# Output projection of a hybrid decoder trunk: its FoX half with seven block products in place of eight

## The chip, the core and the metric

The kernel runs on one core of a Trainium2 chip. The metric is the device time of one execution in microseconds (us), as the median of several runs. A profile of one execution says what each engine did: TensorE (PE, with its weight loads as PEld), VectorE (DVE), ScalarE (ACT), GpSimd (POOL) and the queue SP, which issues most of the DMA transfers.

## The reference

One layer of a decoder trunk, 1024 tokens by 1024 channels, in float32. Cut to what matters here:

```python
def reference(x, p, norm_w, w_in, fox_fb, hgrn_gn, hgrn_lb_logits, w_out, w_ple, w_ple_gate, final_norm_w):
    lb_all = hgrn_lower_bounds(hgrn_lb_logits)
    h = x
    for i in range(DEPTH):                                   # DEPTH = 1
        u = rmsnorm(h, norm_w[i])
        proj = jnp.einsum('bsd,de->bse', u, w_in[i])
        hq, hf, hi, hg, fq, fk, fv, fg, fz = jnp.split(proj, SPLIT_POINTS, axis=-1)
        y_h = hgrn2_branch(hq, hf, hi, lb_all[i], hgrn_gn[i]) * jax.nn.silu(hg)
        y_f = fox_branch(fq, fk, fv, fz, fox_fb[i]) * jax.nn.silu(fg)
        y = jnp.concatenate([y_h, y_f], axis=-1)             # 1024 + 1024 channels
        h = h + jnp.einsum('bse,ed->bsd', y, w_out[i])       # the output projection
        ple = jnp.einsum('bsk,kd->bsd', p[i], w_ple[i])
        h = h + jax.nn.sigmoid(jnp.einsum('bsd,de->bse', h, w_ple_gate[i])) * ple
    return rmsnorm(h, final_norm_w)
```

## The kernel before

Everything is held channels first: a tile has 128 channels as partitions and tokens as columns. The 1024 tokens are worked in two chunks of 512 (`NCH` chunks of `CH`), the channels in eight tiles (`KT`).

To keep float32 precision on TensorE, each operand is split in two parts: a high part (`hi`, a cast by ScalarE, line L82) and a low part (`lo`, source minus high, line L83, by VectorE or GpSimd). Each product of two tiles is three matmuls, high by high (L98), low by high (L99) and high by low (L100); one matmul has 128x128 weights and up to 512 moving columns.

The program's end, where the change lies, has three stages.

1. The HGRN half of the output projection: for each of the eight column tiles `n`, `dense` multiplies the weights of `w_out[n]` by the eight tiles of `y_h` for one chunk after the other (24 matmuls each); `ev_h1` adds x to the result and writes `h[n]` (L1019, VectorE). In the same loop the eight tiles of the FoX output `y_f`, which the earlier stage wrote to memory (`yd`), are read back (L1048) and split into `yhi` and `ylo`.
2. The FoX half: for each column tile `n`, `dense` multiplies `w_out[8+n]` by the tiles of `y_f`, and `ev_h` adds the result to `h[n]` (L1026, VectorE) and splits that chunk at once into `hh` and `hl`, the gates' operands (`hm`). The weights of a tile are loaded and split one tile ahead (`load_w`, two buffers `wf`, two pairs `whi`/`wlo`).
3. The gates: for the token ranges 0 to 512, 512 to 768 and 768 to 1024, and for each column tile, `gate` multiplies `w_gate[n]` by the eight tiles of `hm`, applies a tanh form of the sigmoid, adds the embedding term and sums squares; `norm` ends a range. The gate weights' low parts are made by GpSimd (`wlo`, `glo`, L83); those of the first two tiles, during stages 1 and 2, go into the buffers that the loads of `y_f` had used (tag `g` of the pool `g01`).

What sets the order: each engine works through its own queue in a fixed order, and waits there for semaphores of the others. A scheduler of the framework writes these queues from the program; what is marked to be kept in program order (`pe`, `pin`) stays as written. A buffer of a pool is given out again in turn, and its new writer waits for the old readers. The tiles `hm` use the 32 buffers (tag `u`) that held `y_h`.

Of the kernel before, what the change touches and what calls it, by code (L numbers as in the profile page):

```python
# [64 lines left out]
def trunk(ctx: ExitStack, tc: tile.TileContext, a, out):  # L65
    nc = tc.nc
    mm = nc.tensor.matmul
# [13 lines left out]
    def split(hi, lo, src, lo_engine, pin=lambda ins: ins):  # L81
        pin(nc.scalar.copy(hi, src))  # L82
        pin(lo_engine.tensor_tensor(out=lo, in0=src, in1=hi, op=ALU.subtract))  # L83

    def load_w(src, k, lo_engine=None, pin=lambda ins: ins):

        wf = wpool.tile([P, KT, P], F32, name="wf", tag="wf", bufs=2)
        nc.sync.dma_start(out=wf[:, :k], in_=src)
        hi = wpool.tile([P, KT, P], F32R, name="whi", tag="whi")
        lo = wpool.tile([P, KT, P], F32R, name="wlo", tag="wlo")  # L90
        split(hi[:, :k], lo[:, :k], wf[:, :k], lo_engine or nc.gpsimd, pin)
        return hi, lo

    def product(ps, terms, pin=lambda ins: ins):

        n = len(terms)
        for i, (whi, wlo, uhi, ulo) in enumerate(terms):
            pin(mm(ps, whi, uhi, start=i == 0, stop=False))  # L98
            pin(mm(ps, whi, ulo, start=False, stop=False))  # L99
            pin(mm(ps, wlo, uhi, start=False, stop=i == n - 1))  # L100
# [57 lines left out]
    with ExitStack() as st:  # L158
# [61 lines left out]
        acc = sp.tile([P, S], F32, name="acc")  # L220
# [47 lines left out]
        u = operands("uhi", "ulo")  # L268
# [27 lines left out]
        for c in range(NCH):  # L296
            for k in range(KT):
# [6 lines left out]
                if c == 0 and k in (2, 4, 6, 7):  # L304
                    i = 8 + (2, 4, 6, 7).index(k)
# [59 lines left out]
    pe = tc.keep_in_program_order  # L365
# [142 lines left out]
    with ExitStack() as st:  # L508
# [269 lines left out]
    with fox as st:  # L778
# [219 lines left out]
        for c in range(NCH):  # L998
            sl = slice(c * CH, (c + 1) * CH)
# [4 lines left out]
    with ExitStack() as st:  # L1004
        hpool = st.enter_context(tc.tile_pool(name="h", bufs=1, side="right", reuse_waits="tile"))
        g01 = st.enter_context(tc.tile_pool(name="g01", bufs=4, reuse_waits="tile"))
        eps_ = st.enter_context(tc.tile_pool(name="eps", bufs=2, space=PSUM, reuse_waits="tile"))
# [4 lines left out]
        h = [h_pair[n // 2][:, n % 2] for n in range(KT)]  # L1012

        def ev_h1(n):
            def ev(c, ps):
                sl = slice(c * CH, (c + 1) * CH)
                x = g01.tile([P, CH], F32, name="xr", bufs=2)
                nc.sync.dma_start(out=x, in_=a["xT"][n][:, sl])
                nc.vector.tensor_tensor(out=h[n][:, sl], in0=ps, in1=x, op=ALU.add)  # L1019

            return ev

        def ev_h(n):
            def ev(c, ps):
                sl = slice(c * CH, (c + 1) * CH)
                nc.vector.tensor_tensor(out=h[n][:, sl], in0=ps, in1=h[n][:, sl], op=ALU.add)  # L1026
                split(*hm[c][n], h[n][:, sl], nc.vector)

            return ev

        def load_gate(n, pool, names, **tag):
            wf = wpool.tile([P, KT, P], F32, name="wf", tag="wf", bufs=2)
            nc.sync.dma_start(out=wf, in_=a["w_gate"][n])
            hi, lo = (pool.tile([P, KT, P], F32R, name=name, **tag) for name in names)
            split(hi, lo, wf, nc.gpsimd)
            return hi, lo

        gw = [None] * KT
        with tc.tile_pool(name="yp", bufs=2 * KT, reuse_waits="tile") as yp:

            y_f = [[] for _ in range(NCH)]
            w = [first_w, load_w(a["w_out"][1], KT, nc.vector, tc.keep_in_program_order)]
            for n in range(KT):
                dense(None, y_h, ev_h1(n), w=w[n])
                w.append(load_w(a["w_out"][n + 2], KT, nc.vector, tc.keep_in_program_order))
                hi, lo = (yp.tile([P, S], F32R, name=name, tag="y") for name in ("yhi", "ylo"))
                y = g01.tile([P, S], F32, name="yf", tag="g")
                nc.sync.dma_start(out=y, in_=yd[KT + n])  # L1048
                split(hi, lo, y, nc.vector, tc.keep_in_program_order)
                for c in range(NCH):  # L1050
                    y_f[c].append(tuple(t[:, c * CH : (c + 1) * CH] for t in (hi, lo)))
            for n in range(2):
                gw[n] = load_gate(n, g01, ("ghi", "glo"), tag="g")

            hm = operands("hh", "hl")
            for n in range(KT):
                dense(a["w_out"][KT + n], y_f, ev_h(n), lo_engine=nc.vector, w=w[KT + n] if n < 2 else None)


        gp = st.enter_context(tc.tile_pool(name="gp", bufs=1, reuse_waits="tile"))  # L1060
# [51 lines left out]
        for t0, t1 in ((0, 512), (512, 768), (768, 1024)):  # L1112
            acc = gp.tile([P, t1 - t0], F32, name="acc", bufs=2)
# [53 lines left out]
```

## Time and profile before

| what | value |
|---|---|
| median of 3 runs | 1309.99 us (1309.87 to 1310.46) |
| the profiled execution's own time | 1311.11 us |
| its span, first to last instruction | 1309.4 us |
| mean granted TensorE clock | 0.996 |
| TensorE busy | 1268.6 us, 97% of the span |
| VectorE, ScalarE, GpSimd busy | 787.7, 475.9, 348.8 us |
| FoX half of the output projection | from 1116.1 to 1203.2 us of the span |

A row of a group of instructions names the line, the engine, the operation, output and inputs with buffer numbers left out, the shape, and how often; then busy time and mean, and how long the engine was idle just before and who ended that. A row of the timeline begins with the start and the duration in us. Stretches of the span ("windows") give busy time per engine, the granted TensorE clock (1.00 is full speed), the share of the DMA engines and what they moved.

### The profile page before, as it was taken

Reading aid. Unit: us, or ns where it says so; the run is one execution under the profiler, and the core shown is the slowest. Engines: PE = TensorE matmul, PEld = TensorE weight load, DVE = VectorE, ACT = ScalarE, POOL = GpSimd, SP = SyncE. Lnnn points to the kernel's source line nnn. Section 1 sums busy time; section 2 is a strip of 40 time slices with the busy share of each in tenths; the row PEclk is TensorE's granted clock in tenths of the full one; section 3 lists DMA queues with packets and bytes.
Section 4 is the critical chain, followed back from the end, with each engine's and each line's share of the span. In section 5 each row is a group of like instructions: output and inputs, shape, how many; then the busy total and the mean of one; then the engine's idle time right before and its main releaser. Section 6 shows DMA issues by size and latency. Waiting matters only on the chain.

```text
span 1309.4 us, 26795 instructions
## 1 busy us (share of the span) xinstructions
PE 1268.6 (97%) x10996; PEld 1014.2 (77%) x10996; DVE 787.7 (60%) x1986; ACT 475.9 (36%) x1146; POOL 348.8 (27%) x288
## 2 busy tenths in 40 slices
PE   7999999999999999999999999999999999999995
PEld 5978888888888878776777777776666788888895
DVE  6556575656647475377666665667777733333465
ACT  6423122222313124344444444444545412222454
POOL 3523113112211112433343424232422200102232
PEclk9999999999999999999999999999999999999998
DMA  7411111201111011222222222211232652212321
GB/s 298 141 38 60 50 49 50 66 18 57 42 50 50 20 66 32 83 60 65 66 74 61 71 69 65 71 58 58 81 114 73 221 183 95 81 49 79 116 80 65
DMA packets 38970, 102.22 MB, mean 78 GB/s; under 512 B 6720, under 2 KB 8896, under 8 KB 38848
## 3 DMA queue, kind: packets, MB, share of 16 engines
q1 hardware_dynamic: 38704, 99.99, 22.9%
q8 instruction: 86, 1.41, 0.4%
q0 software_dynamic: 144, 0.52, 0.1%
q14 instruction: 36, 0.29, 0.1%
HBM read 83.07 MB, written 17.43 MB: 77 GB/s over the span
## 4 chain that ended last, share of the span: by engine, by line
PE 82%; DVE 7%; ACT 6%; DMA 2%; issue 2%; POOL 1%; SPq 0%; DVEq 0%; ACTq 0%; POOLq 0%
PE ps L371 47%; PE ps L100 5%; PE lg L823 5%; PE ps L98 5%; PE ps L99 5%; PE po L871 4%; ACT x L859 2%; PE ps L578 1%; PE gps L99 1%; PE gps L98 1%; PE gps L100 1%; PE po L721 1%; PE po L719 1%; DVE x L837 1%; DMA wf<-in_w_in_dram 1%
## 5 line engine op out<-in xcount | busy, mean ns | idle before, releaser
L371 PE MATMUL ps<-uhi,whi 128*128 128x512 f32 x896 | 360.0, 402 | 0.0
L371 PE MATMUL ps<-ulo,whi 128*128 128x512 f32 x896 | 354.3, 395 | 0.0
L371 PE MATMUL ps<-uhi,wlo 128*128 128x512 f32 x896 | 352.6, 393 | 0.0
L83 POOL TENSOR_TENSOR wlo<-wf,whi 128x1024 fp32r<-128x1024 f32 x59 | 145.3, 2462 | 452.8 <-ACT whi L82 423.4
L371 PEld LDWEIGHTS ps<-uhi,whi 128*128 128x128 f32 x896 | 168.2, 188 | 58.5 <-issue 21.6
L371 PEld LDWEIGHTS ps<-uhi,wlo 128*128 128x128 f32 x896 | 168.4, 188 | 35.6 <-issue 1.1
L371 PEld LDWEIGHTS ps<-ulo,whi 128*128 128x128 f32 x896 | 168.4, 188 | 33.5 <-issue 0.7
L82 ACT CAST whi<-wf 128x1024 fp32r<-128x1024 f32 (+1 forms) x77 | 79.7, 1036 | 206.3 <-PE ps L99 90.0
L859 ACT ACTIVATE x<-x,mxo 128x512 f32<-128x512 f32 (+15 forms) x256 | 130.4, 512 | 66.2 <-DVE mxo L847 66.2
L837 DVE CUSTOM_DVE_ANT_0 x<-lg,fb 128x512 f32<-128x512 f32 (+15 forms) x256 | 101.7, 434 | 78.3 <-PE lg L823 71.4
L860 DVE STREAM_TRANSPOSE pt<-x 128x512 f32<-128x512 f32 (+15 forms) x256 | 115.1, 457 | 38.0 <-ACT x L859 33.9
L98 PE MATMUL ps<-yhi,whi 128*128 128x512 f32 x256 | 99.8, 390 | 1.7 <-DVE h L1019 1.7
L99 PE MATMUL ps<-ylo,whi 128*128 128x512 f32 x256 | 99.7, 389 | 0.4 <-DVE ylo L83 0.4
L100 PE MATMUL ps<-yhi,wlo 128*128 128x512 f32 x256 | 99.6, 389 | 0.0
L823 PE MATMUL lg<-k,q 64*32 64x480 f32 (+15 forms) x1024 | 74.4, 396 | 2.6 <-DVE mx L837 2.6
L823 PE MATMUL lg<-k,qx 64*32 64x512 f32 (+15 forms) x1024 | 74.4, 396 | 0.0
L871 PEld LDWEIGHTS po<-pt,v 64*64 64x64 f32 x1536 | 53.8, 133 | 23.0 <-issue 9.2
L871 PE MATMUL po<-pt,v 64*64 64x256 f32 (+7 forms) x1536 | 69.9, 321 | 0.0
L98 PEld LDWEIGHTS ps<-yhi,whi 128*128 128x128 f32 x256 | 48.0, 188 | 12.2 <-ACT whi L82 2.1
L99 PEld LDWEIGHTS ps<-ylo,whi 128*128 128x128 f32 x256 | 48.0, 188 | 10.6 <-DVE ylo L83 0.8
L100 PEld LDWEIGHTS ps<-yhi,wlo 128*128 128x128 f32 x256 | 48.0, 188 | 10.0
L371 PE MATMUL ps<-wthi,uhi 128*128 128x256 f32 x192 | 54.0, 281 | 0.0
(209 smaller groups left out, 2141.2 us busy)
## 6 DMA issues: line engine op xcount, KB each, us to landing
wf<-in_w_in_dram SPq DMA_DIRECT2D x64, 512.0 KB, 3.5
fb<-fd SPq DMA_DIRECT2D x64, 128.0 KB, 3.2
yf<-yd SPq DMA_DIRECT2D x16, 512.0 KB, 5.9
wf<-in_w_out_dram SPq DMA_DIRECT2D x16, 512.0 KB, 3.6
x<-in_xT_dram SPq DMA_DIRECT2D x8, 512.0 KB, 9.4
pled<-pleo SPq DMA_DIRECT2D x16, 256.0 KB, 2.9
yd<-sg SPq DMA_DIRECT2D x8, 512.0 KB, 2.6
rz<-zd SPq DMA_DIRECT2D x16, 256.0 KB, 3.4
```

The source lines that it names most:

```text
L82: pin(nc.scalar.copy(hi, src))
L83: pin(lo_engine.tensor_tensor(out=lo, in0=src, in1=hi, op=ALU.subtract))
L98: pin(mm(ps, whi, uhi, start=i == 0, stop=False))
L99: pin(mm(ps, whi, ulo, start=False, stop=False))
L100: pin(mm(ps, wlo, uhi, start=False, stop=i == n - 1))
L371: pe(mm(ps, x, y, start=i == j == 0, stop=i == n - 1 and j == 2))
L578: pe(mm(ps[32 * j : 32 * j + 32, c * 48 : c * 48 + 48], k[:, 32 * n : 32 * n + 32], mov(n), start=True, stop=True))
L823: mm(ps[32 * j : 32 * j + 32, m % 2, : 32 * n], q[:, 32 * (j // 2) :][:, :32], k[not own][rows].rearrange("p (t a k) -> p t a k", a=2, k=3 ...
L837: nc.vector.tensor_tensor_reduce(out=x, in0=ps[:, m % 2, : 32 * n], in1=copies[m % 2][:, : 32 * n], scale=1.0, scalar=BIG, op0=ALU.add, op ...
L859: nc.scalar.activation(x, x, AF.Exp, bias=self.other[:, g : g + 1], scale=-1.0, accum_out=zs[:, m : m + 1])
L860: nc.vector.transpose(self.probs[:, : m + 1, g], x.rearrange("p (t k) -> p t k", k=32))
L871: mm(po[half[t % 2], r, 32 * first : 256], v_t[self.p][half[r], t ^ r, half[self.i]], self.probs[half[r], t, first:].rearrange("p g q -> p ...
```

## The change

The first two of the eight column tiles of the FoX half are computed as before. The other six are taken in three pairs. For a pair with the weights a (tile n) and b (tile n+1), each cut by input channel into a first half (tiles 0 to 3) and a second half (4 to 7), and y cut in the same halves and into the two chunks of tokens, the four results (2 tiles x 2 chunks) are a 2x2 block product. Written plainly it has eight block products of 4 x 3 = 12 matmuls. The changed kernel uses seven (the Strassen-Winograd form): it forms four sums of blocks of y once, four sums of blocks of weights for each pair, and adds the products together in `h`.

- `sums_y`: for each of four steps k, reads tiles k and k+4 of `y_f` from memory once more (two loads of 512 KB), forms four differences of 128x512 (`tf`; two by VectorE, two by GpSimd) and splits each (cast by ScalarE, low part by VectorE) into `thi` and `tlo`. These take the 32 buffers `u`. The `tf` share three buffers (tag `t`) with `xr` of stage 1, which had two of its own.
- `Seven(n)`: loads the raw weights of a pair into the two buffers `wf`, and forms `s12` and `s34` (four VectorE operations of 128x512, tag `g`). `parts` splits a raw or summed tile into `whi` and `wlo` (still two pairs of buffers; four such tiles w1 to w4 in a pair).
- `run`: the seven products p1, p6, p2, p5, p7, p3, p4, each in one of four PSUM banks, and after each the additions to `h` (VectorE, three a pair by GpSimd from the SBUF tile `acc`). The next pair's loads and sums are written between p7 and p3.
- The gates' operands `hm` are no longer split behind each result. Their 32 buffers are those of `thi`/`tlo`, which are read until the last pair's products are done; `gate_operands` splits them in four groups within the last pair. The loads of the first two gate weights stand behind the last pair, since `s12` and `s34` use their buffers.

The diff, cut:

```diff
         def ev_h1(n):
...
-                x = g01.tile([P, CH], F32, name="xr", bufs=2)
+                x = g01.tile([P, CH], F32, name="xr", tag="t", bufs=3)
...
                 nc.vector.tensor_tensor(out=h[n][:, sl], in0=ps, in1=h[n][:, sl], op=ALU.add)
-                split(*hm[c][n], h[n][:, sl], nc.vector)
...
+        def sums_y(t):
+            for k in range(KT // 2):
+                b1, b2 = (g01.tile([P, S], F32, name="yf", tag="g") for _ in range(2))
+                nc.sync.dma_start(out=b1, in_=yd[KT + k])
+                nc.sync.dma_start(out=b2, in_=yd[KT + KT // 2 + k])
+                b11, b12, b21, b22 = b1[:, :CH], b1[:, CH:], b2[:, :CH], b2[:, CH:]
+                f1, f2, f3, f4 = (g01.tile([P, CH], F32, name="tf", tag="t", bufs=3) for _ in range(4))
+                minus(f1, b12, b11)
+                minus(f2, b22, f1)
+                split(*t[0][k], f2, nc.vector)
+                split(*t[1][k], f1, nc.vector)
+                minus(f3, b22, b12, nc.gpsimd)
+                split(*t[2][k], f3, nc.vector)
+                minus(f4, b21, f2, nc.gpsimd)
+                split(*t[3][k], f4, nc.vector)
...
+            def run(self, w1, w2, t, following, done):
+                nat = [[y_f[c][KT // 2 * r : KT // 2 * r + KT // 2] for c in range(NCH)] for r in range(2)]
+                p1 = self.times(w1, 0, nat[0][0])
+                acc = g01.tile([P, CH], F32, name="acc", tag="t", bufs=3)
+                nc.scalar.copy(acc, p1)
+                self.add(0, 0, p1)
+                p6 = self.times(w2, 0, t[0])
+                nc.vector.tensor_tensor(out=acc, in0=p6, in1=acc, op=ALU.add)
+                self.add(0, 1, acc, nc.gpsimd)
+                done(0)
+                p2 = self.times(w1, 1, nat[1][0])
+                self.add(0, 0, p2)
+                w3 = self.parts(self.s34)
+                p5 = self.times(w2, 1, t[1])
+                self.add(1, 1, p5)
+                self.add(0, 1, p5)
+                done(1)
+                w4 = self.parts(self.raw[1], (1,))
+                p7 = self.times(w3, 0, t[2])
+                nc.vector.tensor_tensor(out=acc, in0=p7, in1=acc, op=ALU.add)
+                self.add(1, 0, acc, nc.gpsimd)
+                self.add(1, 1, acc, nc.gpsimd)
+                done(2)
+                nxt = following and Seven(following)
+                p3 = self.times(w3, 1, nat[1][1])
+                self.add(0, 1, p3)
+                w1 = nxt and nxt.parts(nxt.raw[0])
+                p4 = self.times(w4, 1, t[3])
+                self.add(1, 0, p4)
+                w2 = nxt and nxt.parts(nxt.s12)
+                done(3)
...
-            hm = operands("hh", "hl")
-            for n in range(KT):
-                dense(a["w_out"][KT + n], y_f, ev_h(n), lo_engine=nc.vector, w=w[KT + n] if n < 2 else None)
+            for n in range(2):
+                dense(None, y_f, ev_h(n), w=w[KT + n])
+            t = [[tuple(upool.tile([P, CH], F32R, name=name, tag="u") for name in ("thi", "tlo")) for _ in range(KT // 2)] for _ in range(4)]
+            sums_y(t)
...
+            ready = (
+                [(0, 0), (0, 1), (0, 2), (0, 3)],
+                [(0, 4), (0, 5), (1, 0), (1, 1)],
+                [(1, 2), (1, 3), (1, 4), (1, 5)],
+                [(0, 6), (0, 7), (1, 6), (1, 7)],
+            )
+            seven = Seven(2)
+            w1, w2 = seven.parts(seven.raw[0]), seven.parts(seven.s12)
+            for n in range(2, KT, 2):
+                last = n == KT - 2
+                seven, w1, w2 = seven.run(w1, w2, t, None if last else n + 2, lambda i: gate_operands(*ready[i]) if last else None)
             for n in range(2):
                 gw[n] = load_gate(n, g01, ("ghi", "glo"), tag="g")
```

How the queues move, at the places that the prediction speaks of. First VectorE at the FoX half's start, before: after the last part of y (`ylo`), each result (L1026) is followed by the splits of the gates' operand and of the next weights.

```order
L83 TENSOR_TENSOR ylo_11452<-yf_11453,yhi_11451 128x1024
L1026 TENSOR_TENSOR h0_10902<-ps_11501,h0_10902 128x512
L83 TENSOR_TENSOR hl_11470<-h0_10902,hh_11469 128x512
L1026 TENSOR_TENSOR h0_10902<-ps_11529,h0_10902 128x512
L83 TENSOR_TENSOR wlo_11616<-wf_11613,whi_11615 128x1024
L83 TENSOR_TENSOR hl_11486<-h0_10902,hh_11485 128x512
```

VectorE in the changed kernel, the end of the same stretch: the last step of the sums, with the third of the four results of the two plain tiles among it, up to the split of the first pair's `s12` (`wlo_11690`).

```order
L1031 TENSOR_TENSOR tf_11658<-yf_11654,tf_11657 128x512
L1031 TENSOR_TENSOR ws_11678<-wf_11673,wf_11674 128x512
L1031 TENSOR_TENSOR ws_11678<-wf_11673,ws_11677 128x512
L1026 TENSOR_TENSOR h0_10902<-ps_11509,h0_10902 128x512
L83 TENSOR_TENSOR tlo_11568<-tf_11658,thi_11567 128x512
L83 TENSOR_TENSOR wlo_11684<-wf_11673,whi_11683 128x512
L83 TENSOR_TENSOR tlo_11576<-tf_11657,thi_11575 128x512
L83 TENSOR_TENSOR wlo_11684<-wf_11673,whi_11683 128x512
L83 TENSOR_TENSOR tlo_11584<-tf_11659,thi_11583 128x512
L83 TENSOR_TENSOR tlo_11592<-tf_11660,thi_11591 128x512
L1026 TENSOR_TENSOR h0_10902<-ps_11535,h0_10902 128x512
L83 TENSOR_TENSOR wlo_11690<-ws_11677,whi_11689 128x512 x2
```

From the last result of stage 1 (L1019) to the first of the two operations of that last row, the queue has 31 operations of 128x512 and two of 128x1024; before, the queue from there held one result and one or two splits per chunk.

Then GpSimd, from its last DMA of the FoX stage on, before: the splits of the gate weights alone.

```order
L933 DMA yd_69<-o7_4288 128x1024
L83 TENSOR_TENSOR glo_11460<-wf_11457,ghi_11459 128x1024
L83 TENSOR_TENSOR glo_11466<-wf_11463,ghi_11465 128x1024
L83 TENSOR_TENSOR wlo_11992<-wf_11989,whi_11991 128x1024
L83 TENSOR_TENSOR wlo_11998<-wf_11995,whi_11997 128x1024
```

GpSimd in the changed kernel, from the last subtraction of the sums on:

```order
L1031 TENSOR_TENSOR tf_11660<-yf_11654,tf_11658 128x512
L1083 TENSOR_TENSOR h1_10903<-acc_11708,h1_10903 128x512 x3
L1083 TENSOR_TENSOR h2_10900<-acc_11844,h2_10900 128x512 x3
L83 TENSOR_TENSOR glo_12148<-wf_12145,ghi_12147 128x1024
L1083 TENSOR_TENSOR h3_10901<-acc_11980,h3_10901 128x512
L83 TENSOR_TENSOR glo_12154<-wf_12151,ghi_12153 128x1024
L1083 TENSOR_TENSOR h3_10901<-acc_11980,h3_10901 128x512 x2
L83 TENSOR_TENSOR wlo_12164<-wf_12161,whi_12163 128x1024
L83 TENSOR_TENSOR wlo_12170<-wf_12167,whi_12169 128x1024
```

Eight subtractions of the sums and nine additions of the rounds have come in, and all gate weights' splits stand in the last pair or behind it.

Last VectorE into the gates, before: one split per result, and then the first gate's result (L1078).

```order
L1026 TENSOR_TENSOR h3_10901<-ps_11929,h3_10901 128x512
L83 TENSOR_TENSOR hl_11484<-h3_10901,hh_11483 128x512
L1026 TENSOR_TENSOR h3_10901<-ps_11957,h3_10901 128x512
L83 TENSOR_TENSOR hl_11500<-h3_10901,hh_11499 128x512
L1078 SCALAR_TENSOR_TENSOR g_12053<-g_12053,pl_12026 128x512
```

VectorE in the changed kernel from the result of p7 (L1104) on; `hl_12130` is the low part of the seventh tile of h, first chunk, and the next L1083 is the result of p4, the last product.

```order
L1104 TENSOR_TENSOR acc_11980<-gps_12069,acc_11980 128x512
L83 TENSOR_TENSOR hl_12062<-h0_10902,hh_12061 128x512
L83 TENSOR_TENSOR hl_12086<-h1_10903,hh_12085 128x512
L83 TENSOR_TENSOR hl_12090<-h1_10903,hh_12089 128x512
L1083 TENSOR_TENSOR h3_10901<-gps_12101,h3_10901 128x512
L83 TENSOR_TENSOR hl_12094<-h2_10900,hh_12093 128x512
L83 TENSOR_TENSOR hl_12098<-h2_10900,hh_12097 128x512
L83 TENSOR_TENSOR hl_12130<-h3_10901,hh_12129 128x512
L1083 TENSOR_TENSOR h3_10901<-gps_12115,h3_10901 128x512
L83 TENSOR_TENSOR hl_12134<-h3_10901,hh_12133 128x512
```

The splits that stood behind each result over the whole stage now stand together around the last products; from the result of p2 to `hl_12130` there are 17 operations.

More of the change, by code (lines that the diff above doesn't have):

```diff
@@ L1026, in ev, with minus @@
                 nc.vector.tensor_tensor(out=h[n][:, sl], in0=ps, in1=h[n][:, sl], op=ALU.add)
-                split(*hm[c][n], h[n][:, sl], nc.vector)
             return ev
+        def minus(out, x, y, engine=nc.vector):
+            engine.tensor_tensor(out=out, in0=x, in1=y, op=ALU.subtract)
+        def sums_y(t):
[13 more added lines that the diff above has]
+                split(*t[3][k], f4, nc.vector)
@@ new lines, in trunk, with __init__, parts, times @@
+        class Seven:
+            def __init__(self, n):
+                self.n = n
+                lo, hi = slice(0, KT // 2), slice(KT // 2, KT)
+                self.raw = a_, b_ = [wpool.tile([P, KT, P], F32, name="wf", tag="wf", bufs=2) for _ in range(2)]
+                for i, t in enumerate(self.raw):
+                    nc.sync.dma_start(out=t, in_=a["w_out"][KT + n + i])
+                self.s12, self.s34 = s12, s34 = [g01.tile([P, KT, P], F32, name="ws", tag="g") for _ in range(2)]
+                nc.vector.tensor_tensor(out=s12[:, hi], in0=b_[:, lo], in1=b_[:, hi], op=ALU.add)
+                minus(s12[:, lo], s12[:, hi], a_[:, lo])
+                minus(s34[:, lo], a_[:, lo], b_[:, lo])
+                minus(s34[:, hi], a_[:, hi], s12[:, lo])
+            def parts(self, src, halves=(0, 1)):
+                hi, lo = (wpool.tile([P, KT, P], F32R, name=name, tag=name) for name in ("whi", "wlo"))
+                for x in halves:
+                    sl = slice(x * KT // 2, (x + 1) * KT // 2)
+                    split(hi[:, sl], lo[:, sl], src[:, sl], nc.vector)
+                return hi, lo
+            def times(self, w, x, mov):
+                ps = eps_.tile([P, CH], F32, name="gps", tag="gate", bufs=4)
+                for k in range(KT // 2):
+                    j = x * KT // 2 + k
+                    for i, (y, z) in enumerate(((w[0], 0), (w[0], 1), (w[1], 0))):
+                        pe(mm(ps, y[:, j], mov[k][z], start=k == i == 0, stop=k == KT // 2 - 1 and i == 2))
+                return ps
+            def add(self, n, c, x, engine=nc.vector):
+                hs_ = h[self.n + n][:, c * CH : (c + 1) * CH]
+                engine.tensor_tensor(out=hs_, in0=x, in1=hs_, op=ALU.add)
+            def run(self, w1, w2, t, following, done):
[29 more added lines that the diff above has]
+                done(3)
+                return nxt, w1, w2
@@ L1052, in trunk, with gate_operands @@
             for n in range(2):
+                dense(None, y_f, ev_h(n), w=w[KT + n])
+            t = [[tuple(upool.tile([P, CH], F32R, name=name, tag="u") for name in ("thi", "tlo")) for _ in range(KT // 2)] for _ in range(4)]
+            sums_y(t)
+            hm = [[None] * KT for _ in range(NCH)]
+            def gate_operands(*which):
+                for c, n in which:
+                    hm[c][n] = tuple(upool.tile([P, CH], F32R, name=name, tag="u") for name in ("hh", "hl"))
+                    split(*hm[c][n], h[n][:, c * CH : (c + 1) * CH], nc.vector)
+            ready = (
[4 rows of a table added]
+            )
[5 more added lines that the diff above has]
+            for n in range(2):
                 gw[n] = load_gate(n, g01, ("ghi", "glo"), tag="g")
-            hm = operands("hh", "hl")
-            for n in range(KT):
-                dense(a["w_out"][KT + n], y_f, ev_h(n), lo_engine=nc.vector, w=w[KT + n] if n < 2 else None)
         gp = st.enter_context(tc.tile_pool(name="gp", bufs=1, reuse_waits="tile"))
```

## The prediction

> **What bounds the kernel now.** I read the page's chain first, then the busy time of each engine in the stage that changes, then the vector and GpSimd queues there in order of time.
>
> ```profile
> span 1309.4 us, 26795 instructions
> PE 1268.6 (97%) x10996; PEld 1014.2 (77%) x10996; DVE 787.7 (60%) x1986; ACT 475.9 (36%) x1146; POOL 348.8 (27%) x288
> PE 82%; DVE 7%; ACT 6%; DMA 2%; issue 2%; POOL 1%; SPq 0%; DVEq 0%; ACTq 0%; POOLq 0%
> ```
>
> TensorE carries 82% of the chain that ended last. By stretches of the profile, in us and busy time per engine (PE, PEld, DVE, ACT, POOL, granted clock): the two FoX column tiles that stay, the six that change, and the gates' first part.
>
> ```profile
> 1116.10:1137.90 21.80, 21.80 (x97) 18.03 (x97) 8.36 (x11) 5.87 (x8) 2.40 (x1) 1.00 0.29 95
> 1137.90:1203.20 65.30, 65.30 (x290) 54.06 (x289) 24.07 (x30) 13.17 (x19) 2.39 (x1) 1.00 0.18 57
> 1203.20:1258.00 54.80, 54.80 (x289) 47.35 (x288) 24.37 (x34) 26.57 (x41) 12.41 (x5) 1.00 0.28 96
> ```
>
> TensorE never stops and the others are mostly idle: a matmul less is time less, as long as TensorE still finds its operands. The chain in order of time says how far a delay is carried:
>
> ```profile
> 1258.04 0.13 PE gps L100
> 1258.19 0.39 ACT g L1077
> 1258.59 1.28 ACT L119
> ```
>
> TensorE leads it without a break until 1258, then ScalarE and the vector engine take over from its last result. So a delay, or a gain, gathered by the gates' start reaches the end whole.
>
> Two vector operations that follow consecutive chunks give the pitch:
>
> ```profile
> 1121.56 0.69 DVE L1026 TENSOR_TENSOR h<-ps,h 128x512 f32<-128x512 f32 x1 [2.22 <-PE ps L100]
> 1127.00 0.69 DVE L1026 TENSOR_TENSOR h<-ps,h 128x512 f32<-128x512 f32 x1 [3.37 <-PE ps L100]
> ```
>
> A chunk of 24 matmuls takes 5.44 us, so one of 512 columns 0.2267.
>
> **What is removed.** A pair of column tiles took 4 chunks of 24 matmuls = 96; seven block products of 12 take 84. Three pairs save 36 matmuls: 36 x 0.2267 = 8.2 us, all on TensorE. A product lasts 2.72 us.
>
> **What is added, and its prices.** Vector operations on 128x512:
>
> ```profile
> 1026.75 1.89 DVE L83 TENSOR_TENSOR ylo<-yf,yhi 128x512 fp32r<-128x512 f32 x3
> 1127.86 1.23 DVE L83 TENSOR_TENSOR wlo<-wf,whi 128x1024 fp32r<-128x1024 f32 x1 [0.17 <-ACT whi L82]
> 1129.00 0.68 DVE L83 TENSOR_TENSOR hl<-h,hh 128x512 fp32r<-128x512 f32 x1
> ```
>
> One alone takes 0.69; in a row, one each 0.60 ((1.89 - 0.69) / 2); of 1024 elements 1.14 (1127.86 to 1129.00). ScalarE's cast of 512 and the loads:
>
> ```profile
> 1133.17 0.62 ACT L82 CAST hh<-h 128x512 fp32r<-128x512 f32 x1 [4.82 <-DVE h L1026]
> wf<-in_w_out_dram SPq DMA_DIRECT2D x1, 512.0 KB, 3.6
> yf<-yd SPq DMA_DIRECT2D x7, 512.0 KB, 5.7
> ```
>
> GpSimd's passes of two SBUF operands, and the vector operations that met them:
>
> ```profile
> L806 POOL TENSOR_TENSOR own<-fb,cst x16: 1268/1289/1301, 531.1 to 962.9; 128x512 f32<-128x512 f32 x16
> 1119.52 2.40 POOL L83 TENSOR_TENSOR glo<-wf,ghi 128x1024 fp32r<-128x1024 f32 x1 [4.68 <-ACT ghi L82]
> 1193.23 2.39 POOL L83 TENSOR_TENSOR wlo<-wf,whi 128x1024 fp32r<-128x1024 f32 x1 [71.31 <-ACT whi L82]
> 1193.70 2.47 DVE L83 TENSOR_TENSOR hl<-h,hh 128x512 fp32r<-128x512 f32 x1 [0.73 <-ACT hh L82]
> 1204.11 2.40 POOL L83 TENSOR_TENSOR wlo<-wf,whi 128x1024 fp32r<-128x1024 f32 x1 [8.49 <-ACT whi L82]
> 1205.53 1.53 DVE L83 TENSOR_TENSOR hl<-h,hh 128x512 fp32r<-128x512 f32 x1 [1.68 <-ACT hh L82]
> 1206.47 2.84 POOL L83 TENSOR_TENSOR glo<-wf,ghi 128x1024 fp32r<-128x1024 f32 x1
> ```
>
> This is what decides the case. The vector split at 1193.70 ends at 1196.17, 0.55 us after the GpSimd pass beside it ended (1195.62); that at 1205.53 ends at 1207.06, again 0.55 after (1206.51); and the next GpSimd pass ends 2.25 after that (1209.31). A vector operation with both operands in SBUF and a GpSimd pass take turns: their times add. A blocked GpSimd pass of 1024 adds 2.25, of 512 half of that, 1.13 (alone 1.27 to 1.30). In before this meets slack; the change puts 8 + 9 small passes and the gate weights' splits among vector work that TensorE waits for.
>
> **Head: sums of y.** From the last HGRN evacuation at 1116.1 (one chunk before 1121.56) the vector queue of the changed kernel holds, up to the first half of the split of the weight sums: 31 operations of 512 and two of 1024: 31 x 0.60 + 2 x 1.14 + 0.1 = 21.0 us. Seven of the eight GpSimd subtractions fall among them: 7 x 1.13 = 7.9. Together 28.9, so 1145.0. TensorE reaches the second product's third matmul, the first with that operand, at 1116.1 + 4 x 5.44 + 2.72 + 0.45 = 1141.0. Stall 4.0 us (half of it at the first product already: 25 + 2 vector operations and six passes end at 1140.3, and its third matmul is due at 1138.4). Bounds: 0 if GpSimd costs the vector engine nothing (1137.1); 5.5 if two or three of ScalarE's casts, between difference and split, are waited for besides. I take 4.0: the rows above are the same operations. The eight extra loads of y cost nothing while the queue is this slow: a buffer comes free one step of the sums (some 7 us, 28.9 / 4) before its next user, and a load takes 5.7. They are queued on SP among the loads of x and of w_out, which then go out a few tenths later and are needed 5 us after. Some 20 casts of 0.62 fit beside the 28.9 us. The HGRN half, which now shares three small buffers with the sums, and the products' four PSUM banks in place of two cost nothing: TensorE's operands there don't change.
>
> A sentence of the Trainium skill (SBUF — State Buffer, "Who interferes with whom") says that a vector instruction with at most one SBUF input doesn't contend with GpSimd; the row at 1121.56 agrees (0.69, beside a pass that lasts to 1121.92). Were each of the head's four evacuations from PSUM to fall beside a pass, the stall would by that rule be 4 x 0.60 less, 1.6; the sum doesn't use it, since the queue rarely places them so.
>
> **Two changes of pair.** The next pair's second raw tile is loaded into the buffer that the split of w4 frees. From the fifth product's end: two adds and that split 3 x 0.60 + 0.1, the load, five vector operations and the first half split 6 x 0.60 + 0.1.
>  1.9 + 3.6 + 3.7 = 9.2; two GpSimd adds just ahead hold the first of them some 0.4, handshakes 0.1: 9.7. TensorE has three products and two matmuls, 8.16 + 0.45 = 8.6. Stall 1.1, twice: 2.2 us (bounds 0 and 3: 1.5 each if the load meets another). The rest of a round is hidden: 19 vector operations (11.4 us), 3 GpSimd adds (3.4) and 8 casts and copies within 19 us.
>
> **Tail: into the gates.** Before, only one split stood between the last chunk and the gates, and the first gate used it late. Now 16 splits of h wait for buffers that the products free, and GpSimd's splits of the second to fourth gate weight stand among them, since their buffers come free only now; before, the second ran at 1119.52 and the other two cost TensorE nothing. Let T be TensorE's end of the last product. From the second of this round's natural products, done at T - 10.9 + 0.2, to the low part of h's seventh tile the vector queue holds 17 operations, 10.3 us; GpSimd's three splits and two adds add 3 x 2.25 + 2 x 1.13 = 9.0. That ends at T + 8.6. The first gate needs it at its 20th matmul, T + 4.3. Stall 4.3; behind it the last evacuation, cast (0.62) and split cost 2.0 against three matmuls, 1.3 more. 5.6 us; lower bound 0, if GpSimd gets to its splits later than the vector engine; upper 5.6 plus the cold clock below.
>
> **Sum.** -8.2 + 4.0 + 2.2 + 5.6 = +3.6. The profiled execution took 1311.11 us (span 1309.40 and 1.71 around it), 1.12 above the median of 1309.99; it becomes 1314.7, the median 1313.6. What comes after the gates' first part is the same code, shifted.
>
> **Rivals.** One: the small passes don't block. Then head and tail fall away and the pair changes keep 0.7 each: -8.2 + 1.4 = -6.8, 1303.2, faster. For the head it decides from 3.9 us for the seven passes, 0.55 each: below that TensorE finds its operands (1141.0 - 1116.1 - 21.0). Against it stand the three rows with 0.55 and 2.25; for it only that no 512 pass beside a vector split is among them.
>
> Two: the tail's order goes the other way. If both gate-weight splits come after the low part of h's seventh tile, 4.5 us of GpSimd leave its chain, and the stall is gone but for about 1.3: -8.2 + 4.0 + 2.2 + 1.3 = -0.7, 1309.3, no change. For it: whichever asks first goes first, and the load that GpSimd's split waits for can be late by a microsecond.
>
> Three: the clock. The chip lowered it here after a pause:
>
> ```profile
> 1297.46 0.70 PE L1097 MATMUL ssq<-acc,ones 128*128 128x256 f32 x2 [3.48 <-DVE acc L115]
> 1297.00:1298.00 1.00, 0.54 (x2) 0.30 (x2) 0.61 (x2) 0.98 (x3) 0.00 (x0) 1.00 0.46 156
> 1298.00:1299.00 1.00, 0.16 (x1) 0.00 (x0) 0.93 (x3) 1.00 (x1) 0.00 (x0) 0.80 0.00 0
> 1299.00:1300.00 1.00, 0.81 (x2) 0.50 (x2) 0.14 (x1) 0.67 (x3) 0.00 (x0) 0.50 0.00 0
> 6.08 0.80 PE L98 MATMUL pple<-phi,whi 128*128 128x512 f32 x1 [6.08 <-ACT whi L82]
> ...
> 10.94 0.63 PE L100 MATMUL pple<-phi,wlo 128*128 128x512 f32 x1
> 11.37 0.58 PE L98 MATMUL pple<-phi,whi 128*128 128x512 f32 x1
> ...
> 12.02 0.39 PE L100 MATMUL pple<-phi,wlo 128*128 128x512 f32 x1
> ```
>
> After 3.48 us of idleness, and almost none of work behind it, it fell to 0.5. At the start matmuls came each 0.43 us (10.94 to 11.37) until 11.8, 13 of them from 6.08, 13 x 0.2 = 2.6 lost. If the tail's 4.3 us trips it: 1313.6 + 2.6 = 1316.2. The Trainium skill (TensorE: Matmul & The Clock Gate, "What's actually happening") has the same: half clock after an idle window of about 3.4 us, whose phase runs free; so a stall of 4.3 need not cover one.
>
> **Chances.** Forecast 0.52 (1311.5 to 1315.5 by the bounds of its terms); clock 0.12; tail the other way 0.20; passes that don't block 0.16. 0.2% is 2.6 us, about what a measurement of this kernel can tell from no change. Slower by more: 0.44 of the forecast's and the clock's 0.12, 0.56. Within: 0.08 and 0.19 of the tail's, 0.27. Faster: 0.17. The range leaves out the no-block case and 0.04 above: 1308.0 to 1317.0.
>
> **What would show it.** Right: 36 matmuls of 512 columns fewer; vector splits beside GpSimd subtractions of 1.2 to 1.9 us; TensorE waits of about 2 at the first and 2 at the second product, 1.1 at the first product of the next pairs, and 4 to 6 in the first gate, released by vector splits. Wrong: splits at 0.69 throughout, first gate without waits, or matmuls at 0.43 pitch behind it. The forecast fails most easily in the tail.

## The result, and the profile after

| | median | runs | against before |
|---|---|---|---|
| before | 1309.93 us | 1309.66 to 1310.46 | |
| changed | 1318.56 us | 1317.79 to 1319.15 | 1.0064, 95% interval 1.0049 to 1.0079 |

The changed kernel is 8.6 us slower; 3.6 were forecast, with 1317.0 as the upper end. The profiled execution took 1319.15 us. First the page of the changed kernel: span, busy times, chain that ended last.

```profile
span 1317.3 us, 26887 instructions
PE 1266.1 (96%) x10960; PEld 1008.9 (77%) x10960; DVE 839.5 (64%) x2049; ACT 491.4 (37%) x1180; POOL 375.6 (29%) x305
PE 76%; DVE 10%; ACT 6%; issue 3%; DMA 3%; POOL 2%; SPq 0%; DVEq 0%; ACTq 0%; POOLq 0%
```

The 36 matmuls are gone (10996 to 10960), yet TensorE's busy time fell only from 1268.6 to 1266.1, 2.5 us in place of 8.2: some of those that stayed take longer. The chain has 76% of TensorE in place of 82%, and 10% of VectorE in place of 7. What TensorE waited for between 1105 and 1240 (us in total, times, longest):

```profile
PE gps L1078 <- DVE wlo L83: 4.7, 5, 1.6
PE gps L99 <- DVE hl L83: 4.2, 1, 4.2
PE gps L1078 <- ACT whi L82: 1.0, 1, 1.0
PE gps L98 <- ACT hh L82: 0.5, 1, 0.5
PE ps L99 <- DVE ylo L83: 0.2, 1, 0.2
```

L1078 is the matmul of the seven products. All releasers but two are splits by VectorE, where before TensorE had no such wait. The stages by windows (columns as before; the granted clock is third from the end):

```profile
1138.00:1152.00 14.00, 10.75 (x38) 7.84 (x37) 8.75 (x14) 2.58 (x5) 2.98 (x2) 0.88 0.11 37
1152.00:1212.00 60.00, 53.91 (x234) 43.33 (x233) 47.14 (x59) 21.47 (x36) 21.96 (x12) 1.00 0.27 88
1218.00:1272.00 54.00, 54.00 (x304) 47.29 (x303) 29.70 (x39) 27.36 (x43) 9.33 (x6) 1.00 0.20 69
1145.00:1147.00 2.00, 2.00 (x6) 1.57 (x7) 0.99 (x2) 0.00 (x0) 0.00 (x0) 0.56 0.00 0
1147.00:1149.00 2.00, 2.00 (x7) 1.57 (x6) 0.00 (x0) 0.00 (x0) 0.00 (x0) 0.58 0.00 0
1213.00:1215.00 2.00, 1.48 (x3) 0.78 (x3) 1.32 (x4) 1.95 (x4) 0.00 (x0) 0.63 0.97 349
1215.00:1217.00 2.00, 2.00 (x6) 1.57 (x5) 0.60 (x1) 2.00 (x3) 1.26 (x1) 0.52 0.27 103
```

Twice the clock falls to about half for some 3.4 us: at 1145, where VectorE and TensorE have just got through the sums, and at 1213, in the first gate. From 1218 on TensorE is as full as before. In the timeline the first fall reads so:

```profile
1144.84 0.50 PE L1078 MATMUL gps<-thi,wlo 128*128 128x512 f32 x1 [0.68 <-DVE wlo L83]
1145.18 0.56 PE L1078 MATMUL gps<-thi,whi 128*128 128x512 f32 x1
...
1147.24 0.63 PE L1078 MATMUL gps<-thi,wlo 128*128 128x512 f32 x1
...
1148.82 0.40 PE L1078 MATMUL gps<-yhi,whi 128*128 128x512 f32 x1
```

The start after 1144.84 comes 0.34 later, not 0.2267: each restart costs some 0.25 beyond the wait shown (0.16 ahead of the first start, 0.11 behind it). From 1145.18 to 1148.82 nine starts take 3.64 us and would take 2.04 at the usual pitch: 1.6 lost.

Adding up all that TensorE's starts lie apart beyond 0.2267, in us:

| place | forecast | measured, restarts included |
|---|---|---|
| head: waits of 0.25, 1.61, 0.96, 0.68 | 4.0 | 4.6 |
| first fall of the clock | 0 | 1.6 |
| two pair changes, waits of 1.09 and 1.10 | 2.2 | 2.7 |
| last round's fifth product, wait of 0.19 | 0 | 0.5 |
| first gate, waits of 4.19 and 0.52 | 5.6 | 5.1 |
| second fall of the clock | 0 | 1.8 |

Together 16.3, and 16.3 - 8.2 = 8.1; the span rose by 7.9.

The head in VectorE's and GpSimd's queues:

```profile
1117.75 0.69 DVE L1031 TENSOR_TENSOR tf<-yf 128x512 f32<-128x512 f32 x1 [0.81 <-POOL tf L1031]
1129.16 0.69 DVE L1060 TENSOR_TENSOR ws<-wf 128x512 f32<-128x512 f32 x1 [1.19 <-POOL tf L1031]
1131.73 1.67 POOL L1031 TENSOR_TENSOR tf<-yf,tf 128x512 f32<-128x512 f32 x1 [2.61 <-DVE tlo L83]
1132.17 1.78 DVE L83 TENSOR_TENSOR tlo<-tf,thi 128x512 fp32r<-128x512 f32 x1
1140.54 1.67 POOL L1031 TENSOR_TENSOR tf<-yf,tf 128x512 f32<-128x512 f32 x1 [3.63 <-DVE tlo L83]
1140.99 2.60 DVE L83 TENSOR_TENSOR tlo<-tf,thi 128x512 fp32r<-128x512 f32 x2
1144.11 1.28 DVE L83 TENSOR_TENSOR wlo<-ws,whi 128x512 fp32r<-128x512 f32 x2
```

A split of 0.68 takes 1.78 beside GpSimd's subtraction: 1.10, where 1.13 was forecast. The first half of the split of the weight sums ends at 1144.8, forecast for 1145.0. Not foreseen is that VectorE also stands idle for GpSimd's results, three times, 3.2 us together (two of the rows are shown), because the differences share three buffers. The tail:

```profile
1205.66 5.60 POOL L83 TENSOR_TENSOR wlo<-wf,whi 128x1024 fp32r<-128x1024 f32 x2
1206.78 5.64 DVE L83 TENSOR_TENSOR hl<-h,hh 128x512 fp32r<-128x512 f32 x3
1212.47 0.50 PE L99 MATMUL gps<-hl,ghi 128*128 128x512 f32 x1 [4.19 <-DVE hl L83]
```

Three splits, 1.9 us alone, take 5.64 beside two of GpSimd's passes; the last of them is what the first gate's 20th matmul waits for, the one that the forecast named.

### The profile page after: what moved, and what is told of

Read it like the earlier page. It is cut to its first block, busy times and chain, and to the rows that moved or that the text cites. A ratio compares the mean times of both kernels' runs of the same rounds, so it can differ in the third digit from the quotient of the medians.

```text
span 1317.3 us, 26887 instructions
## 1 busy us (share of the span) xinstructions
PE 1266.1 (96%) x10960; PEld 1008.9 (77%) x10960; DVE 839.5 (64%) x2049; ACT 491.4 (37%) x1180; POOL 375.6 (29%) x305
## 4 chain that ended last, share of the span: by engine, by line
PE 76%; DVE 10%; ACT 6%; issue 3%; DMA 3%; POOL 2%; SPq 0%; DVEq 0%; ACTq 0%; POOLq 0%
PE ps L371 46%; PE lg L823 5%; PE po L871 4%; PE ps L100 2%; ACT x L859 2%; PE ps L98 2%; PE ps L99 2%; PE gps L1078 2%; PE ps L578 1%; PE gps L98 1%; PE gps L99 1%; PE gps L100 1%; PE po L719 1%; PE po L721 1%; DVE x L837 1%
## 5 line engine op out<-in xcount | busy, mean ns | idle before, releaser
L98 PE MATMUL ps<-yhi,whi 128*128 128x512 f32 x160 | 62.5, 390 | 1.8 <-DVE h L1019 1.8
L99 PE MATMUL ps<-ylo,whi 128*128 128x512 f32 x160 | 62.5, 391 | 0.6 <-DVE ylo L83 0.6
L100 PE MATMUL ps<-yhi,wlo 128*128 128x512 f32 x160 | 62.3, 389 | 0.0
L371 PE MATMUL ps<-wtlo,uhi 128*128 128x256 f32 x192 | 54.0, 281 | 0.0
L371 PE MATMUL ps<-wthi,ulo 128*128 128x256 f32 x192 | 54.0, 281 | 0.0
L99 PE MATMUL gps<-hl,ghi 128*128 128x256 f32 (+1 forms) x144 | 46.6, 324 | 4.2 <-DVE hl L83 4.2
```

The costliest lines, as they stand in the source:

```text
L371: pe(mm(ps, x, y, start=i == j == 0, stop=i == n - 1 and j == 2))
```

## The experiments

The theory after the result: each of the forecast's waits is there at about its size, and what failed is the clock. It was told apart from two others: that the falls come with the changed code whatever the waits are, and that the waits are made by something else than the vector queue (too much vector work as such, or transfers). Gaps are counted below as in the table. How much a kernel gains on the changed one is told by its distance to before on its own chip (1309.96 to 1310.09 there), against the changed kernel's 8.6.

**The subtractions to VectorE.** The head alone, without GpSimd.

```diff
-                minus(f3, b22, b12, nc.gpsimd)
+                minus(f3, b22, b12)
-                minus(f4, b21, f2, nc.gpsimd)
+                minus(f4, b21, f2)
```

> The eight subtractions f3 and f4 that GpSimd makes are made by VectorE; nothing else changes. Theory (turns): a GpSimd pass of 512 beside vector work with two SBUF operands costs 1.13 us of the head, a vector operation 0.60, so seven of them save 3.7 us: head stall from 4.6 to about 0.5, and the first fall of the clock (1.6 us) goes with it. 1318.6 - 5.7 = 1312.9 us. Rival (the vector queue itself is the bound, GpSimd runs beside it): eight more operations of 0.60 make the head 4 to 5 us longer, 1323 us.

1313.25 us (ratio 1.0022, 1.0012 to 1.0032): 3.2 over before, a gain of 5.5 on the changed kernel. VectorE does eight operations more and is done sooner. Window of the head, and the two groups of waits that are left:

```profile
1138.00:1152.00 14.00, 14.00 (x62) 11.23 (x61) 9.42 (x16) 3.12 (x6) 1.30 (x1) 1.00 0.15 43
PE gps L99 <- DVE hl L83: 4.1, 1, 4.1
PE gps L1078 <- DVE wlo L83: 2.2, 2, 1.1
```

The head's waits and its fall of the clock are gone together (clock 1.00, TensorE full). The waits of the pair changes and the tail are unchanged, but the fall in the first gate lasts 6.8 us in place of 3.4, and 3.2 us are lost by it in place of 1.8.

**Differences written in place.** GpSimd keeps its subtractions, but f3 and f4 overwrite their sources, so that the three buffers don't run short.

```diff
-                f1, f2, f3, f4 = (g01.tile([P, CH], F32, name="tf", tag="t", bufs=3) for _ in range(4))
+                f1, f2 = (g01.tile([P, CH], F32, name="tf", tag="t", bufs=3) for _ in range(2))
+                f3, f4 = b12, b21
```

> f3 and f4 are still made by GpSimd, but written over the blocks of y that they are made from (b12 and b21), so that only f1 and f2 take turns in the three small buffers; the next step's f1 no longer waits for GpSimd's f4. Theory (the head's stall is both: 3.2 us of VectorE waiting for GpSimd's result or buffer, the rest taking turns at the port): stall from 4.6 to about 2, the first clock fall (1.6) goes: 1318.6 - 4.2 = 1314.4 us. Rival (port alone): GpSimd's seven passes cost what they cost, no change, 1318 to 1319 us.

1315.60 us (1.0043, 1.0029 to 1.0056): a gain of 3.1, with 1.2 missing to the theory's time. The head's waits shrink to one, so the buffers were a part of it; that the turns with GpSimd are the rest is shown by the subtractions on VectorE, where none is left. Why it fell short:

```profile
1138.44 0.58 PE L1079 MATMUL gps<-yhi,wlo 128*128 128x512 f32 x1 [1.98 <-DVE wlo L83]
1138.83 0.63 PE L1079 MATMUL gps<-yhi,whi 128*128 128x512 f32 x1
...
1141.39 0.63 PE L1079 MATMUL gps<-yhi,whi 128*128 128x512 f32 x1
```

One pause of 1.98 us, with none over 0.25 in the 20 us ahead of it, and the matmuls behind it are slow: durations of 0.63, starts 0.43 apart, 1.7 us lost in all. In the first gate the clock was low for 6.8 us here, too.

**No sums of y.** Leaves out the forming of the sums: the products multiply plain parts of y in their place, so this kernel no longer computes the layer and only shows what the sums cost.

```diff
-            sums_y(t)
+            t = [[y_f[i % 2][KT // 2 * (i // 2) + k] for k in range(KT // 2)] for i in range(4)]
```

> Leaves out forming the sums of y: the products take plain parts of y in their place, so there are no extra loads, differences and splits, and the buffers of the gates' operands are free early. Seven products, weight sums and pair changes stay. Theory (head and tail both hang on the sums and their buffers): head 4.6 and first clock fall 1.6 go, the tail's 5.1 and its clock fall 1.7 go or shrink to about 1; pair changes (2.7) stay. 1318.6 - 12 = 1306.6 us. Rival (the tail hangs on GpSimd's gate weight splits, whatever the buffers): only the head goes, 1318.6 - 6.2 = 1312.4 us. Second rival (seven products cost something by themselves): over 1314 us.

1306.80 us (0.9975, 0.9966 to 0.9985), within 0.2 of the theory. So the seven products do bring what was counted, and with no sums to pay for the change would be faster than before by 3.3. The wait in the tail shrinks as well, to 0.90, without an edit to the splits there, probably since the gates' operands no longer wait for buffers that hold sums. No fall of the clock is left. Its waits for `wlo` are 1.10, 1.09 and 1.07, some 12 to 20 us apart.

**TensorE kept busy.** 38 unused matmuls, put ahead of the waiting ones at the first two products (8, 5, 4) and in the first gate (18, 3).

```diff
                     for i, (y, z) in enumerate(((w[0], 0), (w[0], 1), (w[1], 0))):
+                        if k == 0 and i < len(idle) and idle[i]:
+                            spin(idle[i], gold)
```

> Adds 38 matmuls whose results are not used, in front of the five long TensorE waits (8, 5 and 4 at the first two products, 18 and 3 in the first gate), so that TensorE works where it paused; what it waits for is unchanged. Theory (the clock falls because of the pauses): both falls go, 3.3 us, and the 0.1 to 0.2 us that each restart costs, about 0.7: 1318.6 - 4.0 = 1314.6 us, granted clock 1.00 from 1140 to 1290. Rival (the falls have another cause, or the count of pauses doesn't matter): clock falls remain, 1318 to 1319 us.

1315.52 us (1.0042, 1.0027 to 1.0057): a gain of 3.2, with 38 matmuls more; 0.9 over the theory. The operands come no earlier; what is gone is both falls of the clock (mean clock 0.996 as in before, against 0.993; 1.00 throughout the head and the first gate):

```profile
1203.00:1219.00 16.00, 15.73 (x68) 12.30 (x67) 9.36 (x9) 4.52 (x6) 10.46 (x5) 1.00 0.55 186
```

So the falls follow from the pauses. That they cost the 3.4 us of the table agrees with the gain, but isn't told apart from the restarts, some of which are gone as well.

**Next pair's sums behind the split.** In the pair change, `s12` and `s34` are formed behind the split of the next raw tile, not ahead of it.

```diff
                 w1 = nxt and nxt.parts(nxt.raw[0])
+                nxt and nxt.sums()
```

> The next pair's weight sums are written behind the split of its first raw tile, so that this split, which needs only a tile that is long there, isn't queued behind four sums that wait for the second tile's load. Theory (the pair change is the chain load, sums, split): its 2.7 us for two changes fall to about 0.5, while head, tail and clock falls stay: 1318.6 - 2.1 = 1316.5 us. Rival (TensorE waits there for the buffers of w3 or for the load itself): no change, 1318 to 1319 us.

1316.66 us (1.0049, 1.0034 to 1.0065), as the theory had it; but the four executions took 1314.84 to 1318.02, so the time alone hardly excludes the rival's 1318. The timeline does. A pair change after the edit (the wait was 1.09):

```profile
1164.94 0.50 PE L1082 MATMUL gps<-thi,wlo 128*128 128x512 f32 x1 [0.17 <-DVE wlo L83]
```

The other pair change waits 0.17 as well. The chain of raw load, sums and split was the pair change's limit. The last round's wait grew from 0.19 to 0.42.

**Gates' operands in the order of need.** All eight tiles that the first gate reads are split first.

```diff
                 [(0, 0), (0, 1), (0, 2), (0, 3)],
-                [(0, 4), (0, 5), (1, 0), (1, 1)],
-                [(1, 2), (1, 3), (1, 4), (1, 5)],
-                [(0, 6), (0, 7), (1, 6), (1, 7)],
+                [(0, 4), (0, 5), (0, 6)],
+                [],
+                [(0, 7)] + [(1, n) for n in range(KT)],
```

> The operands of the gates are split in the order in which the gates need them: the first chunk of tiles 0 to 6 in the first two groups, then that of tile 7 and only then the second chunk, which the gates use 43 us later. GpSimd's splits stay where they were. Theory (the tail is the length of the queue ahead of two splits): the tail's 5.1 us fall to 0 or nearly, and the second clock fall (1.7) goes: 1318.6 - 6.8 = 1311.8 us. Rival (GpSimd's gate weight splits block whatever stands there): some 4 us of stall stay, 1317 to 1318 us.

1312.13 us (1.0017, 1.0008 to 1.0026): a gain of 6.5, the largest single mend. The wait of 4.19 became

```profile
1209.84 0.50 PE L99 MATMUL gps<-hl,ghi 128*128 128x512 f32 x1 [1.15 <-DVE hl L83]
```

and the clock stays at 1.00 behind it. The splits of the second token range, which no gate needs for another 43 us (8 x 5.44), had stood ahead of those that were due.

**The gate weights' low parts on VectorE.** The tail's other half: GpSimd no longer splits the first four gate weights.

```diff
-            split(hi, lo, wf, nc.gpsimd)
+            split(hi, lo, wf, nc.vector if n < 2 else nc.gpsimd)
...
-                gw[n] = load_w(a["w_gate"][n], KT) if n < 4 ...
+                gw[n] = load_w(a["w_gate"][n], KT, nc.vector) if n < 4 ...
```

> The low parts of the gate weights 0 to 3 are made by VectorE in place of GpSimd (1.14 us each in place of 2.25 of blocking). Theory (turns): the three that stand in the tail take 3.4 us in place of 6.8, the tail's stall goes from 5.1 to about 1.8, short enough for the clock to stay (1.7): 1318.6 - 5.0 = 1313.6 us. Rival (the tail's length is the vector queue's, GpSimd ran beside it): three operations more, 1318.6 + 3 = 1322 us.

1314.96 us (1.0042, 1.0027 to 1.0057; runs 1314.45 to 1317.55): a gain of 3.8, 1.4 over the theory. The profiled execution is the highest of the four; in it the long wait is split in two, and the clock falls all the same (from 1210.03 to 1216.85):

```profile
1208.80 0.73 PE L98 MATMUL gps<-hh,ghi 128*128 128x512 f32 x2 [1.59 <-ACT hh L82]
1211.05 0.80 PE L99 MATMUL gps<-hl,ghi 128*128 128x512 f32 x1 [1.52 <-DVE hl L83]
1211.00:1213.00 2.00, 1.95 (x5) 1.57 (x6) 1.67 (x3) 1.49 (x2) 0.95 (x1) 0.50 0.84 296
```

The other three took 2.3 to 3.1 us less, at a mean granted clock of 0.994 against 0.991: they had less time at half speed, but where they had it is not recorded.

**Three mends together**: subtractions on VectorE, sums behind the split, operands in the order of need.

> e1, e9 and e11 in one kernel. Theory (the three stalls and the two clock falls are separate and all of what was lost): of the 16.2 us that the pauses took, 0.3 stay at the head, 0.5 at the pair changes, 0.9 in the last round, none in the tail: -8.2 + 1.7 = -6.5, 1303.5 us, faster than before by 0.5%. Rival (a mended place hands its wait to the next one, as the last round's w4 or the gates): 1306 to 1310 us.

1307.51 us (0.9976, 0.9967 to 0.9984): faster than before, but 4.0 over the theory; the mends' gains one by one (5.5, 2.0, 6.5) would have given 1304.6. The rest of the loss is in the first gate:

```profile
1196.52 2.39 POOL L83 TENSOR_TENSOR wlo<-wf,whi 128x1024 fp32r<-128x1024 f32 x1 [0.45 <-ACT whi L82]
1199.95 2.35 POOL L83 TENSOR_TENSOR wlo<-wf,whi 128x1024 fp32r<-128x1024 f32 x1 [1.04 <-ACT whi L82]
1200.43 6.42 DVE L83 TENSOR_TENSOR hl<-h,hh 128x512 fp32r<-128x512 f32 x4 [4.18 <-ACT hh L82]
1202.91 0.50 PE L99 MATMUL gps<-hl,ghi 128*128 128x512 f32 x1 [1.96 <-DVE hl L83]
...
1205.05 0.63 PE L100 MATMUL gps<-hh,glo 128*128 128x512 f32 x1
```

The last split that the gate needs, the first of the row's four, starts half a microsecond after a pass of GpSimd and is held up by it; the wait of 1.96 (0.24 stood ahead of it) lowers the clock. This execution is one of the longer ones: of the eleven, six took 1307.5 to 1307.9 us at a mean clock of 0.994 to 0.995, and five 1304.8 to 1306.4 at 0.995 to 0.996. Probably the fall did not come in those five, but they have no trace. What was gained ahead was partly handed on to this place, as the rival had it: TensorE arrives sooner, and the splits don't.

**Four mends**: these three, and the gate weights' low parts on VectorE.

> The three mends together, and the low parts of the first four gate weights made by VectorE in place of GpSimd. Three pairs, 36 matmuls fewer than before. Theory (the 2.6 us of waits left in the first gate of the kernel with three mends are VectorE's splits held up by GpSimd's passes of 2.25 each): VectorE does them in 1.14 each, the waits fall under 0.6, no clock fall (1.7): 1307.5 - 2.0 - 1.7 = 1303.8. Rival (VectorE simply has too much to do there, whoever makes the low parts; in the changed kernel with this edit alone two pauses of 1.75 and 2.02 stayed in place of 4.34 and 0.68): the waits stay near 2 and the clock falls again: 1307.0.

1303.99 us (0.9954, 0.9941 to 0.9968), the theory's 1303.8. The same place in VectorE's and TensorE's timelines:

```profile
1196.37 1.23 DVE L83 TENSOR_TENSOR wlo<-wf,whi 128x1024 fp32r<-128x1024 f32 x1 [3.26 <-ACT whi L82]
1198.78 1.23 DVE L83 TENSOR_TENSOR wlo<-wf,whi 128x1024 fp32r<-128x1024 f32 x1 [0.59 <-ACT whi L82]
1199.92 2.49 DVE L83 TENSOR_TENSOR hl<-h,hh 128x512 fp32r<-128x512 f32 x4
1200.66 0.50 PE L99 MATMUL gps<-hl,ghi 128*128 128x512 f32 x1 [0.63 <-DVE hl L83]
```

Four splits take 2.49 where they took 6.42, the wait is 0.63, and the clock is 1.00 throughout. The engine that does more work is done sooner, since nothing takes turns with it there.

**Two pairs, then two plain tiles**: with the first two mends, tiles 6 and 7 computed as in before, behind the last pair, and the splits of the gates' operands grouped to suit; 24 matmuls saved.

```diff
-            for n in range(2, KT, 2):
-                last = n == KT - 2
+            for n in (2, 4):
+                last = n == 4
...
+            for n in (6, 7):
+                dense(a["w_out"][KT + n], y_f, ev_h(n), lo_engine=nc.vector)
+                gate_operands((0, n), (1, n))
```

> Two pairs by seven products (tiles 2 to 5), then the last two column tiles plainly, with the sums on VectorE and the next pair's sums behind the split. 24 matmuls fewer than before in place of 36: 24 x 0.2267 = 5.4 us less. Theory (the waits at the gates' start come from the splits of the gates' operands that stand behind the last products; with two plain tiles, 4 x 5.44 = 21.8 us of TensorE work, behind them, they are hidden): one pair change of 0.33 and about 0.3 elsewhere stay, no clock fall: 1310.0 - 5.4 + 0.6 = 1305.2. Rival (what holds the first gate is GpSimd's splits of the gate weights, which stand there whatever ends the output projection): a wait of 2.6 and a clock fall of 1.7 stay as in the kernel with three mends: 1309.5. By the theory it beats that kernel (1307.5) with twelve matmuls more.

1305.88 us (0.9969, 0.9956 to 0.9981), 0.7 over the theory and below the three mends with twelve matmuls more. All that TensorE still waits for from 1105 to 1240:

```profile
PE ps L100 <- DVE wlo L83: 0.2, 1, 0.2
PE gps L1082 <- DVE wlo L83: 0.2, 1, 0.2
```

The plain tiles hide the gates' operands wholly; GpSimd's passes of the gate weights still stand there (one from 1198.95 to 1201.35 beside a split of 1.53), and TensorE waits for none of it.

## Why the prediction was wrong, step by step

- **What is removed, 8.2: right.** Without the sums' cost, or with it hidden, the saving comes through (without the sums -3.3 with 5.2 of gaps left; two pairs -4.1 of 5.4; four mends -6.0 of 8.2).
- **Head, 4.0: size right (4.6 with restarts), mechanism right in part.** That a vector split and a GpSimd pass take turns was read from passes of 1024; those of 512 showed 1.10 for 1.13. But the seven passes did not make 7.9 us of turns: three held up vector work by 1.10 to 1.32 each and one by 0.34, 3.9 us together, and behind the other three VectorE stood idle for their results, 3.2 us, which the working had not seen. That the sum came out alike is luck; moving the subtractions takes both away. The rival of passes that don't block fell. The Trainium skill's rule (SBUF — State Buffer, "Who interferes with whom") that a vector instruction with two SBUF inputs contends with a GpSimd one that reads SBUF agrees: 0.68 became 1.78.
- **Pair changes, 2.2: the wait right to 0.01 each**; 0.5 of restarts was left out.
- **Tail, 5.6: right in place, cause and matmul** (4.19 for 4.3 at the 20th matmul, then 0.52 for 1.3). The close agreement is partly luck: the result of p2, from which the queue was counted, came to VectorE at 1194.65, 9.2 us ahead of the last product's end (T, 1203.8) and not 10.7, since the splits ahead of it were held up by GpSimd too; and the turns behind it cost 7.5 us, not 9.0. The rival of the other order fell here, but the order is indeed what sets it, as the order of need shows.
- **The failed step is the clock, sized at nothing in the sum** and kept as a rival with a chance of 0.12, for the tail only. It came twice and cost 3.4 us. The step's error was to judge by before's pause of 3.48 us and by the idle window of about 3.4 us that the prediction cites, of which it says that a stall of 4.3 "need not cover one", and to ask only of the one long wait. The runs showed that about half of a fixed step of 3.41 us is enough (last section). By that, a pause of 4.3 us leaves at least 2.1 us idle in one step wherever it lies (an estimate from the steps shown there), so the tail's fall was to be expected, and the head's 4.0 us of waits were a risk. The profiled execution was to take 1314.7 and took 1319.15, 4.5 more: 3.4 are the clock, and 1.1 the other rows of the table, mostly restarts (some 0.25 at each wait).

## What to carry to other kernels

A wait on TensorE costs more than its length: price each pause with its restart, and pauses of which some 1.6 to 1.9 us can fall into one 3.41 us step of the clock with a fall of the clock. When a trade gives TensorE less work for more on the engines that feed it, write out those engines' queues at the start and at the end of the stage: there the saved time is lost, and there it comes back by order of need and by work that covers it. Moving work from an idle GpSimd to a busier VectorE can be the faster way, where both read SBUF.

## What the runs showed of the chip

The clock fell here after pauses far shorter than the 3.48 us seen in before. In each of the twelve profiles it changes only at points that lie a whole number of steps of 3.41 us apart: in the changed kernel at 1145.25, 1148.66, 1213.52 and 1216.93, with 19 such steps between the two falls. Here are steps of the changed kernel ahead of and in the falls, and a pause that lowered nothing, in the step from 1036.02 to 1039.44:

```profile
1138.43:1141.84 3.41, 1.93 (x8) 1.61 (x9) 3.41 (x6) 0.00 (x0) 1.30 (x1) 1.00 0.00 0
1141.84:1145.25 3.41, 1.77 (x7) 0.85 (x6) 3.27 (x5) 2.14 (x4) 0.37 (x1) 1.00 0.45 154
1145.25:1148.66 3.41, 3.41 (x10) 2.63 (x9) 0.74 (x2) 0.00 (x0) 0.00 (x0) 0.50 0.00 0
1210.11:1213.52 3.41, 0.73 (x2) 0.30 (x2) 2.91 (x3) 0.47 (x1) 1.16 (x1) 1.00 0.88 302
1213.52:1216.93 3.41, 3.21 (x7) 2.28 (x8) 1.90 (x3) 3.41 (x6) 1.20 (x1) 0.50 0.58 214
1039.10 0.47 PE L98 MATMUL ps<-yhi,whi 128*128 128x512 f32 x1 [1.75 <-DVE h L1019]
```

By these profiles what counts is how much of one step TensorE stands idle, not how long one pause is. At the head it was 1.64 us of a step (3.41 less 1.77), from the pauses of 0.96 and 0.68; the pause of 1.61 lies in the step ahead, which had 1.48 idle, and no fall follows that one. In the first gate it was 2.68. From 25 us of the span on, every step at full speed of the twelve profiles with 1.9 us idle or more was followed by half speed, and none with 1.55 or less; of those between, four were (1.61 to 1.64, at the head, two pauses in each) and nine were not (1.73 to 1.82). So the single pause of 1.98 with the differences in place, which lies within one step, lowered the clock, and six single pauses of 1.49 to 1.73 in before and some fifteen of 1.07 to 1.15 in the changed kernel and six experiments did not.

Half speed held for one step where TensorE was busy through nearly all of it: at each head, in the changed kernel's first gate and in that of the three mends, with 1.6 to 1.8 us lost. It held for two, 6.83 us, with 2.7 to 3.4 lost, where 0.67 us or more of the pause reached into the first: in the first gate with the subtractions on VectorE, the differences in place, the gate weights on VectorE and the sums behind the split. So the size of a fall isn't settled by the wait alone but by where it lies among the steps: a wait of 4.19 cost one step, 4.11 and 3.87 cost two.

The Trainium skill (TensorE: Matmul & The Clock Gate, "What's actually happening") gives two states, half and full, and a free-running window of about 3.4 us: the pitch of 0.43 and the steps of 3.41 agree. That a whole idle window is needed does not: 1.64 us of 3.41 were enough. Its section "A second HAM failure mode: psum-queue depth-cycling" tells of a clock that oscillates through many short idle times, which is nearer to the two short pauses at the head. What decides between 1.6 and 1.9 us stays open.
